# Latent attention: weights times values as one float32 product per key tile, with the sums in the same product

## Chip, cores and metric

The kernel runs on one core of a Trainium2 chip. What is compared is the device time of one execution in microseconds (us), the median of several runs.

## What is computed

The reference is a network of two blocks on 1024 tokens of width 1024. The change touches one part of the second block, an attention of eight heads ("latent", because its keys and values are made from a narrow projection). Each head has 1024 queries and keys of 96 numbers (64 plain, 32 rotated) and values of 64:

```python
def mla_attention(q, k, v):
    ...
    def one_block(q_blk):
        s = jnp.einsum('bqhd,bkhd->bhqk', q_blk, k).astype(jnp.float32) * scale
        p = jax.nn.softmax(s, axis=-1).astype(v.dtype)
        return jnp.einsum('bhqk,bkhd->bqhd', p, v)
    ...

def second_block(...):
    ...
    out_a = mla_attention(q, k, v).reshape(B, S, MLA_WIDTH)
    ...
    out_b = dilated_attention(partial_rope(dq), partial_rope(dk), dv.reshape(B, S, DIL_HEADS, DIL_HEAD_DIM))
    ...
    mixed = jnp.einsum('bsc,cd->bsd', jnp.concatenate([out_a, out_b], axis=-1), w_out[l])
    x = x + gt_a * mixed
    ...
    x = x + gt_m * expert_choice_ffn(h2, w_router[l], b_router[l], w_gate[l], w_up[l], w_down[l])
```

## The kernel before

**How the order comes about.** Every piece of work is a generator that issues some instructions and then yields a condition. `Sched.run` asks a record of what was issued so far (`Model`, with a planned clock for each engine) which piece goes next, by priority. The result is a fixed order of instructions for each of five queues: PE (products), DVE (vector), ACT (scalar, exponentials), POOL (GpSimd) and SP (which issues the transfers). Each queue runs in its order and waits on semaphores. All instructions are recorded on one line, L186, so the profile is read by tiles: `blk` is a 4 KB block of the on-chip heap, `hb` a 2 KB one, `ps` one of eight banks for products, `mmx` and `mng` the maxima of the latent attention and their negation, `mrd` the reciprocals of its sums.

**Precision.** A number is usually split into a high and a low part of type float32r (`copy` or `split` makes the high part, a subtraction the low one), and a product of two split operands is three products of parts (`mm3`). The profile shows float32r as f32 too. What tells the two apart there: a product in plain float32 stands as two records, each with its weight load.

**The latent attention** (`mla`, L2447). `mla_make` makes queries, keys and values and writes them to memory. `mla_keys`, `mla_vals` and `mla_queries` load them again and split them. Sixteen units (`mla_unit`, L2323; a head and half of the queries, so 512 queries against 1024 keys) do the rest, up to `MLIVE` = 6 of them begun at once, each with `MRES` = 6 blocks kept back for it:

1. eight products of high parts, 128 queries by 512 keys, whose maxima DVE takes (`top`); negated, they are transposed by four products and copied by ACT into row 96 of the queries, so that the next product subtracts them;
2. for each pair `j` of key tiles two times three products (128 keys by 512 queries, 97 rows with that of the maxima), whose exponentials ACT takes into `e`;
3. POOL adds the exponentials of all key tiles into `acc`, one 128x512 addition for each tile but the first;
4. `e` (128 x 1024) is split: a copy by ACT or DVE, and a subtraction by `lo_any` on DVE or POOL;
5. for each key tile two products with [high | low] values as weights (`mm2`), one pair behind (`MLAG` = 1), all sixteen into one bank;
6. the bank is copied to `ob`; four products of `acc` with ones give the sums, four products with two stacked identities (`fold`) transpose the result and add its halves; DVE takes the reciprocal and multiplies, and the result goes to memory.

The core of steps 3 to 5 before:

```python
            nc.gpsimd.tensor_add(acc, e[:, 0], e[:, 1]) if j == 0 else nc.gpsimd.tensor_add(acc, acc, e[:, 0])
            if j > 0:
                nc.gpsimd.tensor_add(acc, acc, e[:, 1])
            ...
            hl = [R.blk((P, 2, 512), F32R) for _ in range(2)]
            self.copy(hl[0], e)
            yield
            self.lo_any(hl[1], e, hl[0])
```

**What runs beside it.** The dilated attention (`dilated`, `dil_load`, `dil_unit`, `dil_merge`) has a lower priority and fills gaps, up to four of its units at once while the latent attention runs. When both are done, the output projection, the routing of tokens to experts and the experts follow.

Of the kernel before, what the change touches and what calls it, by code (L numbers as in the profile page):

```python
# [9 lines left out]
F32 = mybir.dt.float32  # L10
# [9 lines left out]
P = 128  # L20
# [16 lines left out]
MRES = 6  # L37
# [55 lines left out]
FE = 1000.0  # L93
# [14 lines left out]
# ---------------------------------------------------------------- the order of the instructions  # L108
class Model:
    """What the instructions issued so far occupy: it decides which piece of work is issued next."""  # L110
# [109 lines left out]
class Sched:  # L220
# [16 lines left out]
    def run(self):  # L237
        """until all but the background is done"""
# [122 lines left out]
# ---------------------------------------------------------------- memory and arithmetic  # L361
class Base:
# [70 lines left out]
    def copy(self, out, src):  # L433
        """on whichever of the two engines is free first"""
# [22 lines left out]
    def mm2(self, out, v, hi, lo, start, stop):  # L457
        """v = [high | low] of 64 columns: the parts of the sum end up in the two halves of the rows"""
# [24 lines left out]
    def bc_row(self, dst, row, n=1024):  # L483
        """every partition gets the row"""
# [16 lines left out]
    def lo_any(self, out, src, hi):  # L501
        """operands on chip: on whichever of the two engines is through first"""
# [7 lines left out]
class Reserve:  # L510
    """blocks kept back for a piece of work that has begun: it can always go on"""
# [32 lines left out]
class Weights:  # L544
    """Blocks of weights in the order of their use: loaded, then split in two float32r parts."""
# [71 lines left out]
class Block1(Base):  # L617
    # ---- start
# [65 lines left out]
    def mod_dve(self, l, js, wname, bname, wl, vecs):  # L684
        """weighted rows summed on the vector engine, then over the partitions on the tensor engine: 512 columns at a time"""
# [41 lines left out]
    def mod_pool(self, l, js):  # L727
        """rows weighted by the scalar engine and summed on GpSimd, both vectors: 512 columns at a time"""
# [42 lines left out]
    def scale(self, l, v, j, g):  # L771
        """g (1 + scale)"""
# [11 lines left out]
    # ---- norms and transposes of a tile  # L784
    def prenorm(self, x, A, B):
        """(x rstd) A + B"""
# [12 lines left out]
    def transpose_split(self, z, dst):  # L799
        """z [128, 1024] transposed; dst(half) lists (columns of the bank, hi, lo)"""  # L800
# [20 lines left out]
    # ---- projections into the mixer  # L821
# [9 lines left out]
    def proj(self, ps, xT, W, key, nk, n):  # L831
        """a token tile against a block of columns"""
# [19 lines left out]
    def f_evac(self, S, t, pf):  # L852
# [4 lines left out]
        else:  # L857
            # tokens half the sequence apart
# [10 lines left out]
    def f_parts(self, S):  # L869
        """the first steps of the transform over the eight tiles, in place"""  # L870
# [5 lines left out]
        # even: G0, G4, Re G2, -Im G2  # L876
# [6 lines left out]
        # odd: Re G3, Re G1, Im G3, -Im G1  # L883
# [12 lines left out]
    def ug_evac(self, S, t, pu):  # L896
        """twice the gelu; the gate's heads normed"""
# [42 lines left out]
    # ---- spatial gating  # L940
# [23 lines left out]
    def sgu(self, S):  # L964
        """u (w v + b) / 2, in place of u"""
# [22 lines left out]
    # ---- Fourier  # L988
# [8 lines left out]
    def fourier(self, S):  # L997
# [32 lines left out]
        else:  # L1030
# [12 lines left out]
            # part, offset in the table [S | C | -S | -C]: a real part takes [C | -S], an imaginary one [S | C]  # L1043
# [82 lines left out]
    # ---- attention  # L1126
# [10 lines left out]
    def rope(self, out, tmp, src, t, heads):  # L1137
        """out = src cos + swapped src (signed) sin, over heads of 64"""
# [93 lines left out]
    def unit(self, S, C, t, kv, st):  # L1232
        """4 heads of a query tile"""
# [190 lines left out]
    def post(self, x, ys, G):  # L1424
        """x + rmsnorm(y) G, in place of x"""
# [32 lines left out]
    def out_proj(self, seqs, W, l, src, dst):  # L1458
        """merge, project, add to the residual, norm for the feed-forward"""
# [88 lines left out]
    # ---- feed-forward  # L1548
# [22 lines left out]
    def ff(self, seqs, W, groups, fin, last_group):  # L1571
        """all the tokens against a group of chunks of the hidden width at a time"""
# [75 lines left out]
    def finisher(self, S, l, src, dst, nxt):  # L1648
        """after the feed-forward: residual, and the next norm"""
# [33 lines left out]
    # ---- the block  # L1683
# [68 lines left out]
    def start_mods(self, done):  # L1752
        """scale and shift of the first norms: one on the tensor engine, the other on the vector engine; on every partition"""
# [73 lines left out]
    def start(self, X, C):  # L1827
        """the modulation of the first norms; the tiles of the input"""
# [127 lines left out]
class Block2(Block1):  # L1956
    """proj, latent attention, dilated attention, experts"""

    # ---- rotations from the positions
    def tables2(self):  # L1960
# [14 lines left out]
        def cosine(out, r, tmp):  # L1975
            """sin(pi / 2 - |r|)"""
# [4 lines left out]
        # tokens on the partitions: [cos (32 | 16) | sin, signed]  # L1981
# [22 lines left out]
        # rows 64..95: cosines, 96..127: signed sines; the tokens along the free dimension  # L2004
# [18 lines left out]
    # ---- projections  # L2023
# [35 lines left out]
    def c_evac(self, nm, t, ps):  # L2059
        """norm of a latent, transposed"""  # L2060
# [44 lines left out]
    def passes2(self, X, W):  # L2105
# [19 lines left out]
        for b in range(KB):  # L2125
            for i in range(2):
                k = self.kbuf[b][i]
                self.nc.vector.tensor_scalar(k[96:97, :], self.tabT[96:97, :], 0.0, 1.0 - i, op0=OP.mult, op1=OP.add)
# [5 lines left out]
    # ---- latent attention  # L2134
# [1273 lines left out]
```

## Time and profile before

| | us |
|---|---|
| median of three runs (4331.38 to 4336.57) | 4331.73 |
| span of the profiled execution, first to last instruction | 4329.5 |
| from the first maximum of the latent attention to its last result | 3023 to 3397 |
| rest of the dilated attention, first part of the output projection | 3397 to 3585 |
| end of the output projection, router | 3585 to 3666 |
| sorting for the routing, then gathering the first tokens | 3666 to 3715 |
| experts, end | 3715 to 4329 |

The profiled execution stands in the profile with its span alone; what lies around the span in a run is the difference to the median, 2.2 us. The stages are read from the trace: the maxima `mmx` start at 3023.2 and the last multiplication by `mrd` starts at 3396.9, the last product of the dilated attention with `dw` starts at 3582.6, and the first token gather starts at 3715.1. A view by stages gives for each the busy time of every engine and the granted clock of PE as a share of full speed. A busy PE is not a PE at its peak: its records overlap, and their ends are modelled.

### The profile page before, as it was taken

What the parts mean: (1) busy time and instruction counts of PE and PEld (TensorE: products, weight loads), DVE (VectorE), ACT (ScalarE), POOL (GpSimd) and SP (SyncE); (2) the same over time, 40 slices, a digit from 0 to 9 for tenths busy, and PEclk for the clock granted to TensorE, in tenths of its full rate; (3) what the DMA queues carried; (4) which work ended last, traced back from release to release, by engine and by line L of the source; (5) the groups of instructions that cost most, each with busy time, mean ns of one, the idle gap of its engine ahead of it and who ended that gap; (6) DMA issues with size and microseconds to landing.
All of it is one profiled execution on the core that took longest, in us unless ns stands there. A gap on an engine that the chain in (4) does not pass through costs nothing. (4 is left out here: it accounts for less than half of the span.)

```text
span 4329.5 us, 54977 instructions
## 1 busy us (share of the span) xinstructions
PE 4034.2 (93%) x19984; PEld 3295.4 (76%) x19984; DVE 2780.2 (64%) x5030; ACT 1825.5 (42%) x3699; POOL 769.1 (18%) x853
## 2 busy tenths in 40 slices
PE   7998999999999979989999999798888898699997
PEld 3777778878887869878888888687676787587776
DVE  6447875666666385777233333814788776888898
ACT  3236643221221233564321222413455653687876
POOL 2111130000000061212000000401567424100001
PEclk8999999999999989999999999899889899799999
DMA  6202322233434240133111112423211345799998
GB/s 220 88 23 79 122 81 89 84 103 118 129 116 126 79 148 22 40 122 112 44 45 44 59 44 81 132 70 95 65 34 30 93 128 195 278 350 369 380 368 304
DMA packets 318761, 552.98 MB, mean 128 GB/s; under 512 B 93117, under 2 KB 177365, under 8 KB 318490
## 3 DMA queue, kind: packets, MB, share of 16 engines
q1 hardware_dynamic: 309130, 515.39, 34.9%
q0 software_dynamic: 9360, 34.08, 2.8%
q8 instruction: 157, 2.57, 0.2%
q14 instruction: 114, 0.93, 0.1%
HBM read 488.42 MB, written 60.97 MB: 127 GB/s over the span
## 5 line engine op out<-in xcount | busy, mean ns | idle before, releaser
L186 PE MATMUL ps<-blk 128*128 128x512 f32 (+3 forms) x16104 | 3542.5, 377 | 84.1 <-DVE blk L186 55.8
L186 PEld LDWEIGHTS ps<-blk 128*128 128x128 f32 (+1 forms) x16104 | 2847.1, 192 | 654.4 <-DVE blk L186 87.6
L186 DVE TENSOR_TENSOR blk<-blk 128x1024 fp32r<-128x1024 f32 (+7 forms) x808 | 922.9, 1182 | 139.1 <-ACT blk L186 126.0
L186 ACT CAST blk<-blk 128x1024 fp32r<-128x1024 f32 (+3 forms) x679 | 661.2, 1022 | 662.3 <-DMA blk<-in_w_ff_dram 390.3
L186 DVE TENSOR_TENSOR blk<-blk,ps 128x512 f32<-128x512 f32 (+1 forms) x488 | 324.8, 675 | 326.5 <-PE ps L186 324.9
L186 ACT CAST blk<-ps 128x512 fp32r<-128x512 f32 (+5 forms) x608 | 275.0, 480 | 441.7 <-PE ps L186 420.9
L186 PE MATMUL ps<-ident,blk 128*128 128x128 f32 (+1 forms) x2024 | 327.9, 296 | 113.6 <-DVE blk L186 53.4
L186 POOL TENSOR_TENSOR blk<-blk 128x1024 f32<-128x1024 f32 (+3 forms) x120 | 252.9, 2113 | 1004.4 <-DMA blk<-in_g_post_ff_dram 647.0
L186 DVE TENSOR_TENSOR blk<-ps,blk 128x512 fp32r<-128x512 f32 (+7 forms) x702 | 349.7, 532 | 108.9 <-ACT blk L186 83.1
L186 PEld LDWEIGHTS ps<-ident,blk 128*128 128x128 f32 x2024 | 261.8, 161 | 178.1 <-ACT blk L186 52.0
L186 ACT ACTIVATE hb<-ps 128x512 f32<-128x512 f32 (+2 forms) x194 | 106.5, 549 | 523.3 <-PE ps L186 512.5
L186 DVE SCALAR_TENSOR_TENSOR hb<-hb,cT 128x512 f32<-128x512 f32 x224 | 164.2, 749 | 112.5 <-DMA hb<-in_w_ada_dram 111.0
L186 ACT ACTIVATE blk<-blk,z 128x256 f32<-128x256 f32 (+2 forms) x406 | 214.4, 532 | 46.3 <-DVE z L186 41.3
L186 DVE CAST blk<-hb 128x512 fp32r<-128x512 f32 (+2 forms) x127 | 48.9, 389 | 262.6 <-ACT hb L186 258.0
L186 ACT ACTIVATE blk<-ps 128x512 f32<-128x512 f32 (+1 forms) x198 | 117.4, 598 | 187.6 <-PE ps L186 182.8
L186 ACT ACTIVATE hb<-hb 128x512 f32<-128x512 f32 (+5 forms) x386 | 176.1, 484 | 37.8 <-DVE hb L186 16.8
L186 ACT ACTIVATE blk<-blk 128x1024 f32<-128x1024 f32 (+4 forms) x157 | 117.4, 751 | 162.7 <-DVE blk L186 141.8
L186 ACT COPY blk<-ps 128x512 f32<-128x512 f32 (+2 forms) x131 | 77.2, 596 | 250.5 <-PE ps L186 250.4
L186 POOL TENSOR_TENSOR hb<-hb,blk 128x512 f32<-128x512 f32 x96 | 170.1, 1771 | 26.6 <-ACT blk L186 20.4
L186 DVE SCALAR_TENSOR_TENSOR blk<-blk,z 128x1024 f32<-128x1024 f32 (+2 forms) x146 | 155.0, 1095 | 21.1 <-POOL z L186 20.3
L186 DVE CAST blk<-ps 128x512 fp32r<-128x512 f32 (+2 forms) x178 | 93.5, 545 | 106.1 <-ACT blk L186 53.3
L186 POOL TENSOR_SCALAR sinkb<-sinkb 128x8 f32<-128x8 f32 x2 | 0.5, 245 | 888.8 <-DMA sinkb<-in_sink_dram 888.8
(150 smaller groups left out, 2060.6 us busy)
## 6 DMA issues: line engine op xcount, KB each, us to landing
blk<-in_w_ff_dram SPq DMA_DIRECT2D x128, 512.0 KB
blk<-in_w_gate_dram SPq DMA_DIRECT2D x128, 512.0 KB
blk<-in_w_up_dram SPq DMA_DIRECT2D x128, 512.0 KB
blk<-in_w_down_dram SPq DMA_DIRECT2D x128, 512.0 KB
hb<-in_w_ada_dram SPq DMA_DIRECT2D x208, 256.0 KB
blk<-in_w_ada_dram SPq DMA_DIRECT2D x40, 512.0 KB
blk<-in_w_in_dram SPq DMA_DIRECT2D x36, 512.0 KB
xd<-blk SPq DMA_DIRECT2D x32, 512.0 KB
```

The lines of the kernel that those rows point to most:

```text
L186: return f(*a, **k)
```

## The change

The exponentials are not split. Each key tile takes one float32 product, with the values as weights (66 columns: 64 values and two columns of ones), and row 64 of the result holds the sums. So `acc` and its additions, the split of `e`, the split of the values, the products with ones and the folds go; four transposes of 66 rows take the place of the folds. The values come by heads, eight transfers instead of four, up to four heads ahead. The low parts of queries and keys no longer have a row 96 (the second and third product of the scores read 96 rows), so the clearing of that row by POOL goes. A unit keeps three blocks back instead of six, and counts as ended (`st["live"]`) a step earlier.

```diff
-MRES = 6
+MRES = 3
...
 def mla_vals(self):
...
-            vs = [R.blk((P, 8, 2, 64), F32R) for _ in range(2)]
-            for h, v in enumerate(vs):
-                self.copy(v[:, :, 0], f[:, :, h * 64:(h + 1) * 64])
-            yield
-            for h, v in enumerate(vs):
-                self.lo_any(v[:, :, 1], f[:, :, h * 64:(h + 1) * 64], v[:, :, 0])
...
+        for h in range(8):
+            yield lambda: self.vn == 8 and h < self.hfree + 4 and self.room(2)
+            v = self.blk((P, 8, 66))
+            nc.sync.dma_start(v[:, :, 0:64], self.vd[:, h * 64:(h + 1) * 64].rearrange("(t p) c -> p t c", p=P))
+            nc.vector.memset(v[:, :, 64:66], 1.0)
+            yield
+            self.vm.append(v)
...
 def mla_queries(self):
...
-                nc.gpsimd.memset(q[96:97, 1].bitcast(F32), 0.0)
...
 def mla_unit(self, h, half, st, R):
...
-        acc = self.hb()
...
-            if i == 0:
-                return
-            nc.gpsimd.tensor_add(acc, e[:, 0], e[:, 1]) if j == 0 else nc.gpsimd.tensor_add(acc, acc, e[:, 0])
-            if j > 0:
-                nc.gpsimd.tensor_add(acc, acc, e[:, 1])
-            if self.whole(FE):
-                pend[j] = [e]
-                return
-            yield lambda: R.room(2)
-            hl = [R.blk((P, 2, 512), F32R) for _ in range(2)]
-            self.copy(hl[0], e)
-            yield
-            self.lo_any(hl[1], e, hl[0])
-            R.free(e)
-            yield
-            pend[j] = hl
+            if i:
+                pend[j] = e
...
-                    self.mm3(ps, tuple(x[0:97, k] for x in kb), tuple(x[0:97, :] for x in qb), True, True)
+                    for n, (x, y, m) in enumerate(((0, 0, 97), (0, 1, 96), (1, 0, 96))):
+                        nc.tensor.matmul(ps, kb[x][0:m, k], qb[y][0:m, :], start=n == 0, stop=n == 2)
...
-                    if len(hl) == 1:
-                        nc.tensor.matmul(po, v.bitcast(F32), hl[0][:, i], start=x == 0, stop=x == 7)
-                    else:
-                        self.mm2(po, v, hl[0][:, i], hl[1][:, i], x == 0, x == 7)
-                R.free(*hl)
+                    nc.tensor.matmul(po[:66, :], self.vm[h][:, x], e_[:, i], start=x == 0, stop=x == 7)
+                R.free(e_)
...
-        self.copy(ob, po)
+        self.copy(ob[:66, :], po[:66, :])
         self.unbank(po)
+        st["live"] -= 1
+        yield
+        yield lambda: self.banks(2)
         pd = self.bank()
         for i in range(4):
-            nc.tensor.matmul(pd[:, 256 + 2 * i:258 + 2 * i], acc[:, i * P:(i + 1) * P], self.ones, start=True, stop=True)
-        self.freeh(acc)
+            nc.tensor.transpose(pd[:, i * P:i * P + 66], ob[:66, i * P:(i + 1) * P], self.ident[:66, :66])
         yield
         rd = self.sm(4, "mrd", 3)
-        nc.vector.reciprocal(rd, pd[:, 256:264].rearrange("p (i q) -> p i q", q=2)[:, :, 0])
-        for i in range(4):
-            self.fold(pd[:, i * 64:(i + 1) * 64], ob[:, i * P:(i + 1) * P])
-        st["live"] -= 1
...
+        pv = pd.rearrange("p (i c) -> p i c", c=P)
+        nc.vector.reciprocal(rd, pv[:, :, 64])
```

**Where instructions move.** The order of every engine is the same as before up to the first unit's maxima, and again from the sorting on; between them the scheduler, which reckons a float32 product at twice the time of two float32r ones, makes another order. On PE, around the unit of head 4 and second half, before: the four transposes of its maxima, then its scores (`blk`, three for each key tile) mixed with products with values (`blk`, four for a pair of key tiles) of its own and of the unit before it, whose products with ones (`ones,hb`) and folds (`ident_76,hb`) stand between, and transposes of the dilated attention (`identr,blk`).

```order
L186 MATMUL ps<-ident,mng 1x128 x4
L186 MATMUL ps<-blk 128x512 x5
L186 MATMUL ps<-identr,blk 128x128 x8
L186 MATMUL ps<-blk 128x512 x17
L186 MATMUL ps<-ones,hb 128x2 x4
L186 MATMUL ps<-blk 128x512 x3
L186 MATMUL ps<-ident_76,hb 128x64 x4
L186 MATMUL ps<-blk 128x512 x22
L186 MATMUL ps<-ident,mng 1x128 x4
L186 MATMUL ps<-blk 128x512 x20
```

The same place after: `66x512` are the float32 products with values, `ident,hb 128x66` the new transposes, `128x256` and `ident,blk` the dilated attention.

```order
L185 MATMUL ps<-ident,mng 1x128 x4
L185 MATMUL ps<-ident,blk 128x128 x8
L185 MATMUL ps<-blk 128x512 x13
L185 MATMUL ps<-blk 66x512 x2
L185 MATMUL ps<-blk 128x512 x6
L185 MATMUL ps<-blk 66x512 x2
L185 MATMUL ps<-blk 128x512 x6
L185 MATMUL ps<-blk 66x512 x4
L185 MATMUL ps<-blk 128x512 x5
L185 MATMUL ps<-ident,hb 128x66 x4
L185 MATMUL ps<-blk 128x512 x2
L185 MATMUL ps<-blk 128x256 x8
```

A unit's scores and its products with values now stand in one row, with no other unit's between them; the maxima of the next two units, the transposes of the result and pieces of the dilated attention stand at the seam between two units.

On POOL, in the same part of the program, before: additions into `acc` (`hb<-hb,blk`, and `hb<-blk` for a unit's first), clearing of row 96 (MEMSET), and the rotation of the queries (`32x512`).

```order
L186 TENSOR_TENSOR hb<-blk 128x512
L186 TENSOR_TENSOR hb<-hb,blk 128x512 x2
L186 TENSOR_TENSOR hb<-hb 32x512
L186 TENSOR_TENSOR hb<-hb,blk 128x512 x4
L186 MEMSET blk 1x512
L186 TENSOR_TENSOR blk<-blk 128x8x64
L186 TENSOR_TENSOR hb<-hb 32x512
L186 TENSOR_TENSOR hb<-blk 128x512
L186 TENSOR_TENSOR blk<-blk 128x8x64
L186 TENSOR_TENSOR hb<-hb,blk 128x512 x6
```

The same part after, with splits of the queries (`96x512`) and of the dilated attention's values (`128x8x64`):

```order
L185 TENSOR_TENSOR blk<-hb,blk 96x512
L185 TENSOR_TENSOR hb<-hb 32x512
L185 TENSOR_TENSOR blk<-hb,blk 96x512
L185 TENSOR_TENSOR blk<-blk 128x8x64
L185 TENSOR_TENSOR hb<-hb 32x512
L185 TENSOR_TENSOR blk<-hb,blk 96x512
```

The seven additions of each unit are gone from POOL, and what is left is two short instructions for each unit and the dilated attention's splits.

## Rows read from the trace of the kernel before

**Rows 1.** Stages; us; PE, PEld, DVE, ACT, POOL busy (instructions); granted clock; DMA; GB/s.
```profile
2060.00:2690.00 630.00, 630.00 (x2781) 521.65 (x2780) 195.75 (x266) 144.32 (x203) 0.30 (x1) 1.00 0.16 50
...
3023.00:3397.00 374.00, 319.02 (x1461) 251.16 (x1461) 301.53 (x441) 204.58 (x367) 240.15 (x150) 0.89 0.17 41
3397.00:3585.00 188.00, 173.37 (x1127) 157.70 (x1127) 142.21 (x414) 111.80 (x303) 53.28 (x31) 0.91 0.49 137
3585.00:3666.00 81.00, 79.18 (x437) 67.37 (x438) 54.79 (x132) 29.43 (x59) 37.17 (x28) 0.97 0.53 191
...
3715.00:4329.00 614.00, 577.82 (x2712) 467.63 (x2712) 537.72 (x579) 473.15 (x619) 61.81 (x50) 0.98 0.93 346
```

**Rows 2.** Waits in 3023 to 3397: engine, for whom; total us, times, longest.
```profile
PEld ps L186 <- DVE blk L186: 46.8, 41, 4.5
PE ps L186 <- DVE blk L186: 32.2, 29, 4.1
...
PE ps L186 <- DVE mrd L186: 10.5, 9, 2.5
```

**Rows 3.** Groups of 3023 to 3397: DVE, ACT and POOL work; busy us, mean ns.
```profile
L186 POOL TENSOR_TENSOR hb<-hb,blk 128x512 f32<-128x512 f32 x96 | 170.1, 1771 | 26.6 <-ACT blk L186 20.4
L186 DVE TENSOR_TENSOR blk<-blk 128x1024 fp32r<-128x1024 f32 x67 | 112.6, 1685 | 9.9 <-ACT blk L186 9.4
...
L186 DVE TENSOR_REDUCE mmx<-ps 128x1 f32<-128x512 f32 x128 | 82.4, 678 | 6.9 <-PE ps L186 6.7
...
L186 ACT ACTIVATE blk<-ps 128x512 f32<-128x512 f32 x128 | 75.7, 598 | 85.2 <-PE ps L186 81.6
L186 ACT CAST blk<-blk 128x1024 fp32r<-128x1024 f32 x50 | 52.1, 1047 | 0.7
...
L186 POOL TENSOR_TENSOR hb<-blk 128x512 f32<-128x512 f32 x16 | 25.3, 1581 | 70.0 <-ACT blk L186 57.6 <-issue 8.0 <-DMA hb<-mq 4.2
```

**Rows 4.** DVE's costliest group in 2060 to 2690, where POOL is idle.
```profile
L186 DVE TENSOR_TENSOR blk<-blk 128x1024 fp32r<-128x1024 f32 x58 | 69.8, 1223 | 57.7 <-ACT blk L186 57.7
```

**Rows 5.** PE in order of time, two kinds of products, 512 columns: start, us, records.
```profile
79.67 5.31 PE L186 MATMUL ps<-blk,cT 128*2 128x512 f32 x12
84.91 3.01 PE L186 MATMUL ps<-blk 128*128 128x512 f32 x12
```

**Rows 6.** Groups of PE in 3023 to 3397: records, busy us, mean ns.
```profile
L186 PE MATMUL ps<-blk 128*128 128x256 f32 x112 | 22.0, 333 | 0.0
L186 PE MATMUL ps<-ident,hb 128*128 128x64 f32 x128 | 21.7, 325 | 10.6 <-DVE mrd L186 10.5
L186 PE MATMUL ps<-ones,hb 128*128 128x2 f32 x128 | 18.0, 263 | 3.1 <-POOL hb L186 3.1
```

**Rows 7.** PE in order of time, the small products: start, us, records.
```profile
3250.96 0.95 PE L186 MATMUL ps<-ones,hb 128*128 128x2 f32 x8
3251.77 0.94 PE L186 MATMUL ps<-blk 97*128 97x512 f32 x3
...
3405.98 3.77 PE L186 MATMUL ps<-ident,blk 128*128 128x64 f32 x32
...
3409.90 0.62 PE L186 MATMUL ps<-ident,blk 128*128 128x128 f32 x4
3410.28 0.54 PE L186 MATMUL ps<-identr,blk 128*128 128x128 f32 x4
...
3412.56 2.16 PE L186 MATMUL ps<-blk 128*128 128x256 f32 x16
3414.55 0.80 PE L186 MATMUL ps<-identr,blk 128*128 128x128 f32 x8
```

**Rows 8.** Two tiles' own views: ns least/median/most, of all instances.
```profile
L186 PE MATMUL ps<-blk,cT x128: 592/592/1061, 6.3 to 248.6; 128*2 128x512 f32 x128
...
L186 DVE TENSOR_TENSOR mng<-mmx x16: 131/154/1245, 3050.3 to 3361.0; 128x4 f32<-128x4 f32 x16
...
L186 DVE TENSOR_TENSOR hb<-ps,mrd x16: 410/425/425, 3079.7 to 3396.9; 128x256 f32<-128x256 f32 x16
```

More of the change, by code (lines that the diff above doesn't have):

```diff
@@ L92 @@
 DQ = 3.0
-FE = 1000.0
 FT = 2.0
@@ L2127, in passes2 @@
                 k = self.kbuf[b][i]
-                self.nc.vector.tensor_scalar(k[96:97, :], self.tabT[96:97, :], 0.0, 1.0 - i, op0=OP.mult, op1=OP.add)
+                if i == 0:
+                    self.nc.vector.tensor_scalar(k[96:97, :], self.tabT[96:97, :], 0.0, 1.0, op0=OP.mult, op1=OP.add)
                 if b > 0:
@@ L2284, in mla_vals @@
         nc = self.nc
-        for pr in range(4):
-            yield lambda: self.vn == 8 and 2 * pr < self.hfree + 3 and self.room(3)
-            R = self.reserve(3)
-            f = R.blk((P, 8, P))
-            nc.sync.dma_start(f, self.vd[:, pr * P:(pr + 1) * P].rearrange("(t p) c -> p t c", p=P))
-            yield
-            vs = [R.blk((P, 8, 2, 64), F32R) for _ in range(2)]
-            for h, v in enumerate(vs):
-                self.copy(v[:, :, 0], f[:, :, h * 64:(h + 1) * 64])
-            yield
-            for h, v in enumerate(vs):
-                self.lo_any(v[:, :, 1], f[:, :, h * 64:(h + 1) * 64], v[:, :, 0])
-            self.free(f)
-            R.close()
-            yield
-            self.vm += vs
+        for h in range(8):
[3 more added lines that the diff above has]
+            nc.vector.memset(v[:, :, 64:66], 1.0)
+            yield
+            self.vm.append(v)
     def mla_queries(self):
@@ L2362, in mla_unit @@
         pend = {}
-        yield lambda: self.roomh(1)
-        acc = self.hb()
         def expo(ps, e, i, j):
@@ L2401, in mla_unit @@
                     po = self.bank()
-                hl = pend.pop(j - MLAG)
+                e_ = pend.pop(j - MLAG)
                 for i in range(2):
                     x = 2 * (j - MLAG) + i
-                    v = self.vm[h][:, x].rearrange("p a d -> p (a d)")
-                    if len(hl) == 1:
-                        nc.tensor.matmul(po, v.bitcast(F32), hl[0][:, i], start=x == 0, stop=x == 7)
-                    else:
-                        self.mm2(po, v, hl[0][:, i], hl[1][:, i], x == 0, x == 7)
-                R.free(*hl)
+                    nc.tensor.matmul(po[:66, :], self.vm[h][:, x], e_[:, i], start=x == 0, stop=x == 7)
+                R.free(e_)
                 yield 0
@@ L2420, in mla_unit @@
         yield
-        pr = h // 2
         yield lambda: self.roomh(1) and self.banks(2)
         ob = self.hb()
-        self.copy(ob, po)
+        self.copy(ob[:66, :], po[:66, :])
         self.unbank(po)
+        st["live"] -= 1
+        yield
+        yield lambda: self.banks(2)
         pd = self.bank()
         for i in range(4):
-            nc.tensor.matmul(pd[:, 256 + 2 * i:258 + 2 * i], acc[:, i * P:(i + 1) * P], self.ones, start=True, stop=True)
-        self.freeh(acc)
+            nc.tensor.transpose(pd[:, i * P:i * P + 66], ob[:66, i * P:(i + 1) * P], self.ident[:66, :66])
         yield
         rd = self.sm(4, "mrd", 3)
-        nc.vector.reciprocal(rd, pd[:, 256:264].rearrange("p (i q) -> p i q", q=2)[:, :, 0])
-        for i in range(4):
-            self.fold(pd[:, i * 64:(i + 1) * 64], ob[:, i * P:(i + 1) * P])
-        st["live"] -= 1
-        yield
-        nc.vector.tensor_mul(ob[:, 0:256].rearrange("p (q d) -> p q d", d=64), pd[:, 0:256].rearrange("p (q d) -> p q d", d=64),
-                             rd[:, :, None].to_broadcast([P, 4, 64]))
+        pv = pd.rearrange("p (i c) -> p i c", c=P)
+        nc.vector.reciprocal(rd, pv[:, :, 64])
+        nc.vector.tensor_mul(ob[:, 0:256].rearrange("p (q d) -> p q d", d=64), pv[:, :, 0:64], rd[:, :, None].to_broadcast([P, 4, 64]))
         self.unbank(pd)
```

1 line of the change is left out of this document (removed).

## Prediction

> **What bounds the kernel now.** I read the stages first, then who waits for whom, then single groups. The table of stages [rows 1] shows where the change lies: from 3023 to 3397 us, 374 us long. In 2060 to 2690 PE is busy all the time at a granted clock of 1.00; in the 374 us it is busy for 319.0, DVE for 301.5, POOL for 240.2, ACT for 204.6, at a clock of 0.89. So neither PE nor DVE fills the stage: PE waits 55 us in all. What it waits for is mostly DVE: 32.2 us on PE and 46.8 on its weight loads (the two overlap) end with a `blk` that DVE wrote, a low part [rows 2]. And DVE is slow there: a 128x1024 subtraction takes 1685 ns [rows 3], against 1223 ns in the stage in which POOL does nothing [rows 4]. The subtraction of two four-number columns `mng<-mmx` shows the same: 131 ns at the least, 1245 at the most [rows 8]. I read this as DVE held up while POOL works, above all on its additions into `acc`.
>
> The stage's PE work at full clock, worked out to compare with afterwards. A 512-column float32r product takes 630/2781 = 0.2265 us [rows 1]. By the program there are 867 of them (16 units of 8 + 24 + 16, and 99 for the queries): 196.4. The 136 narrower ones of the dilated attention (112 of them are the row in [rows 6]) cost 1.99/16 = 0.124 [rows 7]: 16.9. The 128 records with ones [rows 6] cost 0.81/8 = 0.10 [rows 7]: 13.0. Folds: 128 records [rows 6] and 18 of the dilated attention at 3.77/32 = 0.118 [rows 7]: 17.2. The 200 transposes cost 0.38/4 = 0.095 [rows 7]: 19.0. Sum 262.5 us. So 111 of the 374 us are lost, 55 as idle time, some 41 to the clock (11% of 374), the rest in the ends of products before waits.
>
> **The change part by part.**
>
> *Products with values.* For each of 128 key tiles (16 units of 8) two float32r products, 2 x 0.2265 = 0.453, become one float32 product. The trace has such products: 512 float32 columns with weights of two columns, two records for each, 12 records in 84.91 - 79.67 = 5.24 us [rows 5], so 0.873 a product. That is 0.420 more, times 128: **+53.8 us of PE work**. From below this is firm, since 512 columns stream in both. From above, weights of 66 columns might not load behind the records; the bound is the median of a single record, 592 ns [rows 8], 1.184 a product, +39.8 us more. I take the stream, since 128-column weights load behind 0.2265 us products without a gap in 2060 to 2690 [rows 1]. [...]
>
> *Sums and folds.* The records with ones go, -13.0. The 128 fold records (15.1) become 64 transposes (6.1): -9.0. The transposes of 66 rows have no row; at the price of a fold record they would cost 1.5 more, which I leave to the range. PE's work so rises by 53.8 - 13.0 - 9.0 = **+31.8**.
>
> *Split and additions.* DVE loses nearly all 64 subtractions, 64 x 1.685 = 108, and the 15 copies that ACT did not take; ACT loses 49 copies of 1.047, 51 us; POOL loses 112 additions, 170.1 + 25.3 = 195 us [rows 3]. What stays is under 180 us for DVE, 155 for ACT, 40 for POOL. None of this comes off the time by itself: it takes away what PE waited for, and PE with some 300 us becomes the bound.
>
> *Small edits in one go.* Eight value loads instead of four, and eight clearings of two columns on DVE: the stage's DMA share is 0.17 [rows 1], and values come up to four heads ahead, so nobody waits; at zero cover each load would cost a few us, once. The clearing of row 96 leaves POOL. The 96 rows instead of 97 I take as nothing, since the 512 columns stay. Fewer reserved blocks let more of the dilated attention in.
>
> *The order.* It moves dilated work into the stage: by the program 24 float32r transposes, 24 folds and 12 instructions of dilated units, 2.3 + 5.7 + 1.3 = 9.3 us of PE. And 24 products of the output projection (5.4 us) fall behind the dilated attention's end.
>
> *The seam.* A unit's scores and products with values now stand without another unit's between. ACT keeps up inside: eight exponentials of 0.598 = 4.8 us [rows 3] beside 24 x 0.2265 + 8 x 0.873 = 12.4 us of PE. [...] PE has 3 to 5 us of its own in most seams (maxima of the next units, transposes, dilated products). I take 2 us of loss for a unit, idle time and ends of products together: 32 us. It lies between 0.5, if all is covered, and 4, if nothing is. The clock I take at 0.97: 10 us; it was 0.97 in 3585 to 3666 with PE busy 98% and 0.91 in 3397 to 3585 with 92% [rows 1].
>
> **The sum.** The stage then lasts 262.5 + 31.8 + 9.3 + 32 + 10 = 345.6, against 374: -28.4. The next stage, 188 us, loses 9.3 + 5.4 = 14.7 of PE work; it takes 188/173.4 us for each busy one [rows 1], so -16. The output projection's 24 products come back behind it: +5.4. After that the order is unchanged, and the experts (577.8 of 614 us PE, DMA 0.93 [rows 1]) only begin earlier. Together **-39 us**, on a span of 4329.5, which lies 2.2 us under the median of the runs, 4331.7. I predict 4293 us.
>
> **Rivals.**
>
> *The clock stays at 0.89.* For it: the loss to the clock does not follow the busy share alone, and the seams' transposes and short products are still there. Then the stage loses 303.6/0.89 - 303.6 = 37.5 us to the clock instead of 10: 4293 + 27 = 4320. [...] Against it: twelve us of products without a break in each unit.
>
> *The seam is not covered; slower.* One mechanism: the next unit's maxima are reduced on DVE (0.678 each [rows 3]) behind the dilated attention's work, and PE, with nothing of another unit's to do, waits for the negated maximum. Before, two units' products lay mixed and covered this. The price is up to 6 us a seam, 96 instead of 32: 4293 + 64 = 4357. It turns the result slower from 374 + 10.6 - 303.6 - 10 = 71 us, 4.4 us a unit. For it: order and waits are fixed by planned times, not by real ones. Against it: DVE, with under 180 us of work in 346, is rarely behind.
>
> *The float32 product costs more.* With weight loads not hidden, up to 1.184 each, +39.8 us: 4333, no change. For it: the row has weights of two columns. Against it: see above.
>
> **How the numbers follow.** Forecast 0.64, clock 0.16, seam 0.10, dear product 0.10. A measurement of this kernel can tell about 0.2% (8.7 us) from no change: faster is under 4323. The forecast gives 0.62 of faster and the clock rival 0.10, the dear product, which is not likely to cost its whole bound, 0.02: 0.74. Within 0.2%: 0.14, from the rest of these. Slower: the seam and a little of the dear product, 0.12. The range reaches from 4264 (seams wholly covered and a full clock, -29) to 4332, just short of the dear product's end; out of it are the seam rival and the tails, 2 in 10.
>
> **What would show it.** In the changed profile: the records of `66x512` start 0.44 us apart (not 0.59); no additions on POOL, and 128x1024 subtractions nearly gone from DVE; maxima to last multiplication by `mrd` about 346 us (over 385 would be the seam); granted clock there near 0.97 rather than 0.89; PE's waits for DVE's `blk` under 20 us, its waits at the seams (for `mng`, for ACT's row) 1 to 2 us a unit; sorting begins some 39 us earlier, and the experts' stage still lasts 614 us. The prediction is wrong in its core if PE is busy under 85% of that stage.

## Result: 4274.5 us, 1.4% faster; the profile after

The changed kernel takes 4274.45 us (median of four runs, 4273.72 to 4281.4). The kernel before, run beside it, took 4334.15 (4331.38 to 4343.1). The ratio is 0.986, with a 95% interval from 0.9847 to 0.9873, so -60 us; the profiled spans differ by 57.4 (4329.5 and 4272.1). Forecast were -39.

Stages of the changed kernel (us; then busy time and instructions of PE, PEld, DVE, ACT and POOL; the granted clock; DMA share; GB/s). They answer to the last four rows of [rows 1]; the sorting, left out there, is left out here too ("...").

```profile
3018.60:3354.60 336.00, 321.15 (x1361) 204.49 (x1359) 157.16 (x381) 163.88 (x333) 42.11 (x33) 0.99 0.22 52
3354.60:3525.30 170.70, 153.97 (x1012) 140.69 (x1010) 129.58 (x386) 104.88 (x295) 42.95 (x24) 0.92 0.49 131
3525.30:3609.00 83.70, 81.44 (x434) 68.50 (x435) 57.60 (x127) 29.29 (x57) 35.90 (x27) 0.98 0.60 206
...
3658.50:4272.00 613.50, 577.12 (x2712) 466.90 (x2712) 537.35 (x579) 472.94 (x619) 61.72 (x50) 0.98 0.93 346
```

The latent stage is 38 us shorter, and what PE does in it has turned round: 321.15 of 336.00 us busy at a clock of 0.99, instead of 319.0 of 374 at 0.89. So PE's idle time falls from 55 to 15 us, and what the clock costs (the missing share times the stage) from some 41 to 3 us: about as much comes back through the clock as through the idle time itself. DVE's busy time is about half of before, POOL's a sixth. The experts' stage has the length it had.

Waits of PE and of its weight loads in the latent stage after (us in total, times, longest), in answer to [rows 2]; "issue" is time with no wait that the profile shows (PE is idle for 15 us in all, so some 45 of these 59.8 or more pass while PE is busy):

```profile
PE ps L185 <- ACT blk L185: 11.0, 11, 1.7
PE ps L185 <- DVE blk L185: 1.6, 3, 0.7
...
PE ps L185 <- DVE mng L185: 0.3, 1, 0.3
...
PEld ps L185 <- issue: 59.8, 212, 0.6
PEld ps L185 <- ACT blk L185: 32.3, 71, 2.2
PEld ps L185 <- DVE blk L185: 3.3, 9, 1.0
```

PE's wait for DVE's `blk` is down to 1.6 us, and 3.3 for its weight loads; it was 32.2 and 46.8. What is waited for now is a `blk` of ACT, eleven times on PE and 11 us in all.

Groups of the same stretch (busy us, mean ns of one; idle time before, and what ended it), in answer to [rows 3], [rows 6] and [rows 8]:

```profile
L185 PE MATMUL ps<-blk 128*66 128x512 f32 x256 | 118.1, 593 | 0.0
...
L185 DVE TENSOR_REDUCE mmx<-ps 128x1 f32<-128x512 f32 x128 | 81.6, 682 | 114.2 <-PE ps L185 114.0
...
L185 DVE TENSOR_TENSOR hb<-ps,mrd 128x256 f32<-128x256 f32 x16 | 6.8, 425 | 1.7 <-DVE mrd L185 0.2
```

The 256 records of the first row are the 128 float32 products. DVE waits for PE, 114 us before the maxima alone; before, PE waited for DVE. What a float32 product costs in the row is read from a timeline of PE (start, us from the first start to the last end, records):

```profile
3184.09 12.72 PE L185 MATMUL ps<-blk 97*128 97x512 f32 x40
3196.65 0.60 PE L185 MATMUL ps<-ident,mng 128*1 128x128 f32 x4
```

One unit's scores and products with values, without a break: 24 records of scores and 16 of float32 products, begun 3184.09 and followed at 3196.65, so 12.56 us. With 24 x 0.2265 = 5.44 for the scores, 7.12 us remain for 16 records: 0.445 each, 0.89 a product. The 66-row transposes go four in 0.22 us:

```profile
3174.78 0.42 PE L185 MATMUL ps<-ident,hb 66*128 66x66 f32 x4
3175.00 0.94 PE L185 MATMUL ps<-blk 96*128 96x512 f32 x3
```

### The profile page after: what moved, and what is told of

It reads as the page before. It is cut to its first block, busy times and chain, and to the rows that moved or that the text cites. A ratio compares the mean times of both kernels' runs of the same rounds, so it can differ in the third digit from the quotient of the medians.

```text
span 4272.1 us, 54181 instructions
## 1 busy us (share of the span) xinstructions
PE 4026.4 (94%) x19792; PEld 3240.1 (76%) x19792; DVE 2620.3 (61%) x4945; ACT 1776.9 (42%) x3648; POOL 552.9 (13%) x723
## 5 line engine op out<-in xcount | busy, mean ns | idle before, releaser
L185 DVE TENSOR_TENSOR blk<-blk 128x1024 fp32r<-128x1024 f32 (+8 forms) x743 | 815.4, 1139 | 142.0 <-ACT blk L185 135.7
L185 ACT CAST blk<-blk 128x1024 fp32r<-128x1024 f32 (+2 forms) x625 | 608.1, 1025 | 658.6 <-DMA blk<-in_w_ff_dram 370.2
L185 ACT CAST blk<-ps 128x512 fp32r<-128x512 f32 (+4 forms) x610 | 276.8, 482 | 423.2 <-PE ps L185 404.7
L185 POOL TENSOR_TENSOR blk<-blk 128x1024 f32<-128x1024 f32 (+3 forms) x113 | 240.1, 2129 | 1050.4 <-PE ps L185 664.6
L185 DVE CAST blk<-hb 128x512 fp32r<-128x512 f32 (+3 forms) x130 | 49.8, 387 | 260.2 <-ACT hb L185 255.6
L185 DVE CAST blk<-ps 128x512 fp32r<-128x512 f32 (+3 forms) x176 | 91.5, 539 | 105.7 <-ACT blk L185 53.2
L185 DVE TENSOR_REDUCE mmx<-ps 128x1 f32<-128x512 f32 x128 | 81.6, 682 | 114.2 <-PE ps L185 114.0
L185 DVE TENSOR_TENSOR blk<-hb,blk 128x512 fp32r<-128x512 f32 (+5 forms) x224 | 122.1, 557 | 39.4 <-ACT blk L185 36.5
```

Source lines behind the costliest of these rows:

```text
L185: return f(*a, **k)
```

## The experiments

Each kernel ran beside the kernel before, which took 4334 to 4337 us. All times are medians; ratios are to that kernel. "PE's work" is the program's instructions at the prices of [rows 1, 5 to 7], with 0.89 for the float32 product. Three points cut the profiled spans: the first `mmx`, the end of the last multiplication by `mrd`, and the first gather of tokens for the experts. The stretch from the first point to the last is 691.9 us long before and 640.0 after: -51.9.

**The product alone, with POOL's additions left.** The kernel before already has a switch for it:

```diff
-FE = 1000.0
+FE = -1000.0
```

> The kernel before with one part of the change alone: the exponentials are not split, and each key tile takes one float32 product with the [high | low] values; the additions on POOL, the products with ones and the folds stay. Theory A (the split on DVE held PE up; PE bounds the stage without it): most of the gain is there, the records with ones (13 us) and the folds (9 us) still to pay, so 4295 to 4305 us, and the stage some 360 us. Rival B (POOL's additions were the brake, through the DVE instructions that they held up): little gain, 4320 to 4350.

Measured: 4330.79 us, ratio 0.9988 (0.9978 to 0.9998). That is no gain to speak of; the rival had it. The split is gone from DVE and ACT, and the stretch is nearly as long as before (687.4 us): PE has 56 us more to do, and only about as much was won. In the latent stage PE's idle time falls from 55 to 23 us, and the clock rises from 0.89 to 0.94, which is worth some 20. So the float32 product without the columns of ones is not worth its price.

**The additions alone.**

```diff
-            nc.gpsimd.tensor_add(acc, e[:, 0], e[:, 1]) if j == 0 else nc.gpsimd.tensor_add(acc, acc, e[:, 0])
-            if j > 0:
-                nc.gpsimd.tensor_add(acc, acc, e[:, 1])
+            if j == 0:
+                nc.gpsimd.memset(acc, 8.0)
```

> The kernel before without POOL's 112 additions: the array of sums is set to a constant by one instruction a unit, so the result is not divided by the sums; all else stays, split and two products too. Theory A: DVE's 128x1024 subtractions go from 1.69 to about 1.22 us, 30 us off DVE, of which a part reaches PE: 4305 to 4325 us. Rival B: most of the gain, 4280 to 4295, with PE's waits for DVE's blocks under 30 us.

Measured: 4290.56 us, ratio 0.9887 (0.9871 to 0.9904): -45 us. The split, which PE's waits had named, is still there; only POOL's additions are gone. The theory that asked for 4305 to 4325 missed, the rival had it. DVE's groups in the latent stage (3028 to 3347 us here) show one reason:

```profile
L186 DVE TENSOR_TENSOR blk<-blk 128x1024 fp32r<-128x1024 f32 x59 | 76.0, 1291 | 15.6 <-ACT blk L186 15.0
```

The subtraction takes 1291 ns instead of 1685 [rows 3], and PE's waits for DVE's low parts fall to 10.7 us (weight loads 17.6):

```profile
PE ps L186 <- DVE blk L186: 10.7, 10, 3.2
...
PEld ps L186 <- DVE blk L186: 17.6, 21, 3.6
```

**The split alone, with no float32 product.** ACT writes the exponentials as float32r, and both products read them; PE's work stays.

```diff
...
-            hl = [R.blk((P, 2, 512), F32R) for _ in range(2)]
-            self.copy(hl[0], e)
-            yield
-            self.lo_any(hl[1], e, hl[0])
-            R.free(e)
-            yield
-            pend[j] = hl
+            pend[j] = [e, e]
...
-                e = R.blk((P, 2, 512))
+                e = R.blk((P, 2, 512), F32R)
...
```

> The kernel before without the split, at the same PE work: ACT writes the exponentials as float32r, and both products of a key tile take them (the low part is left out, and the high one counted twice, so the result is doubled). POOL's additions, the products with ones and the folds stay. Theory A, as it stands after the first runs (the time is PE's work plus what PE loses; without the split it loses some 59 us less, which the float32 product then spends): 4265 to 4290 us. Rival B (the additions themselves are the brake, not the split): 4315 or more.

Measured: 4345.49 us, ratio 1.0024 (1.0014 to 1.0034): 10 us slower. The work that the waits had named is taken away, and nothing comes of it: the first theory asked for at most 4290. The latent stage of this kernel (3025 to 3406 us) has as much idle PE as before, 55 us, and a lower clock, 0.85; its waits tell where the time went:

```profile
3025.00:3406.00 381.00, 326.15 (x1448) 266.50 (x1448) 160.47 (x354) 158.29 (x316) 188.57 (x152) 0.85 0.16 39
...
PE ps L186 <- POOL hb L186: 39.2, 16, 3.3
...
PEld ps L186 <- POOL hb L186: 45.9, 16, 3.7
```

Sixteen waits, one for each unit, for the accumulator. Timelines of POOL and of PE over one unit of this kernel (start, us, operation; in brackets the idle time before and what ended it):

```profile
3180.67 1.29 POOL L186 TENSOR_TENSOR hb<-blk 128x512 f32<-128x512 f32 x1 [2.94 <-ACT blk L186]
3182.04 8.08 POOL L186 TENSOR_TENSOR hb<-hb,blk 128x512 f32<-128x512 f32 x6
...
3176.63 11.10 PE L186 MATMUL ps<-blk 128*128 128x256 f32 x52
3190.17 1.05 PE L186 MATMUL ps<-ones,hb 128*128 128x2 f32 x8 [2.44 <-POOL hb L186]
```

POOL adds seven times without a pause, 1.35 us each, and ends at 3190.12. PE is through with the products with values 2.44 us earlier and cannot go on: its next instruction is the product with ones, and behind it in the fixed order stand the folds, the products for the maxima of a coming unit, and then the next unit's scores.

The same place in the kernel before, one seam, on POOL, DVE and PE:

```profile
3172.76 8.88 POOL L186 TENSOR_TENSOR hb<-hb,blk 128x512 f32<-128x512 f32 x4 [0.95 <-ACT blk L186]
...
3178.99 1.50 DVE L186 TENSOR_TENSOR blk<-blk 128x1024 fp32r<-128x1024 f32 x1
...
3180.55 0.98 PE L186 MATMUL ps<-blk 128*128 128x512 f32 x3 [0.32 <-DVE blk L186]
3181.70 1.05 PE L186 MATMUL ps<-ones,hb 128*128 128x2 f32 x8 [0.17 <-POOL hb L186]
```

The unit ends in two tails side by side. DVE's last low part is ready at 3180.49 and lets PE's last products go at 3180.55; POOL's last addition ends at 3181.64, and PE's products with ones start at 3181.70. After the wait for the first tail only 0.17 us are left of the second, and so the waits name DVE. Not every seam is like this one: by the same trace the sum is ready less than 0.7 us before the products with ones in eight of the sixteen, and 1.9 to 6.9 us before them in the others.

**Neither split nor additions, PE's work as before.**

```diff
-            nc.gpsimd.tensor_add(acc, ef[0], ef[1]) if j == 0 else nc.gpsimd.tensor_add(acc, acc, ef[0])
-            if j > 0:
-                nc.gpsimd.tensor_add(acc, acc, ef[1])
+            if j == 0:
+                nc.gpsimd.memset(acc, 8.0)
```

(on the kernel without the split)

> The kernel before with neither the split nor the additions, at its PE work: exponentials as float32r, counted twice by the two products, the sums set to a constant by one instruction a unit. So the result is doubled and not divided by the sums. Theory E (after a unit's last exponentials two tails of some 3 us run side by side, the split on ACT and DVE and the last two additions on POOL, and PE waits for the later one, so that either alone hides what the other's removal would bring): far more than the removal of the split alone (which brought nothing) and more than that of the additions alone (45 us): 60 to 85 us off, 4250 to 4275. Rival B (only the additions count): as without the additions, 4283 to 4298.

Measured: 4276.05 us, ratio 0.986 (0.9843 to 0.9876): -61 us against the kernel before, where the split alone gave +10. The time is a microsecond above the theory's range and 7 us under the rival's. In the latent stage PE's idle time falls from 55 us without the split to 26, and the clock rises from 0.85 to 0.93, which is worth some 34 us. By these rows more than half of what the waits at the seams cost is clock:

```profile
3026.00:3351.10 325.10, 299.27 (x1480) 243.26 (x1481) 155.60 (x358) 160.10 (x321) 51.47 (x59) 0.93 0.20 48
```

**The last two additions of a unit alone.** On the same kernel without the split, five of POOL's additions and a clearing stay; only those of the last pair of exponentials go.

```diff
-            nc.gpsimd.tensor_add(acc, ef[0], ef[1]) if j == 0 else nc.gpsimd.tensor_add(acc, acc, ef[0])
-            if j > 0:
-                nc.gpsimd.tensor_add(acc, acc, ef[1])
+            if j < 3:
+                nc.gpsimd.memset(acc, 1.0) if j == 0 else nc.gpsimd.tensor_add(acc, acc, ef[0])
+                nc.gpsimd.tensor_add(acc, acc, ef[1])
```

> The kernel before without its split (ACT writes the exponentials as float32r, both products read them), and of POOL's seven additions a unit only five and a clearing, those of the first three pairs: nothing is added after the last pair of exponentials, so the sums leave out a quarter of the keys and the product is doubled. PE's work is that of the kernel before. Theory E (PE waits at a unit's end for whichever of two tails comes last: the split of the last pair or POOL's two additions of it): with both tails gone PE's 39 + 46 us of waiting for POOL's sum, as seen without the split alone, mostly go: 4285 to 4310. Rival F (it is the mass of POOL's additions that holds up DVE and so PE, wherever they stand): five of seven additions remain, so little changes: 4320 to 4330 or more.

Measured: 4271.88 us, ratio 0.985 (0.9833 to 0.9867): 74 us less than with all seven, more than the theory asked for, with 80 of 112 additions in place. PE's waits for POOL, 3026 to 3290 us of this kernel, and the additions there:

```profile
PE ps L186 <- POOL hb L186: 0.9, 1, 0.9
...
PEld ps L186 <- POOL hb L186: 1.4, 1, 1.4
...
L186 POOL TENSOR_TENSOR hb<-hb,blk 128x512 f32<-128x512 f32 x80 | 106.3, 1329 | 63.6 <-ACT blk L186 58.1
```

That the mass of additions costs the time, wherever they stand, falls as the main cause in the kernel without the split: it is when the sum is ready. With the split, where the additions do slow DVE (1685 ns a subtraction instead of 1291), it stays open how much of the 45 us of the additions alone came from DVE's faster subtractions and how much from the sum. A reservation: the scheduler, which makes a new order for each of these kernels, reckons with the earlier end, and has the dilated attention nearly all behind the latent stage (PE's work in that stage 235 us instead of 260). But the whole stretch from the first maximum to the first gather, which holds the same work in every order, went from 701.7 us to 631.1.

**Is PE the bound after?** One float32r product for a key tile in place of the float32 one; the low parts of exponentials and values are left out.

```diff
-            v = self.blk((P, 8, 66))
...
+            f = self.blk((P, 8, 66))
...
+            v = self.blk((P, 8, 66), F32R)
+            self.copy(v, f)
...
-                e = R.blk((P, 2, 512))
+                e = R.blk((P, 2, 512), F32R)
```

> The changed kernel with float32r exponentials and values, so that each key tile takes one float32r product instead of one float32 product (the low parts are left out, a less exact result). PE loses 128 x (0.89 - 0.2265) = 85 us of work, DVE or ACT gains eight copies. Theory A (PE bounds the stage): 60 to 80 us come off, 4195 to 4215 us. Rival D (the seams, ACT or DVE bound it by now): 30 us or less, 4245 or more.

Measured: 4194.06 us, ratio 0.9669 (0.9653 to 0.9685). PE has 128 x (0.89 - 0.2265) = 85 us less to do, and the time falls by 80. PE bounds the stage. (The stage itself is 115 us shorter; some 18 us of that are work of the dilated attention that moved behind it.) This version beats both kernels, with exponentials and values rounded to float32r, which both kernels avoid. Its latent stage:

```profile
3016.00:3237.30 221.30, 212.13 (x1064) 165.61 (x1065) 143.99 (x332) 141.96 (x289) 37.85 (x29) 1.00 0.28 69
```

**Blocks kept back for a unit.** The prediction priced `MRES` at nothing. The changed kernel with the old value:

```diff
-MRES = 3
+MRES = 6
```

> The changed kernel with six blocks kept back for a unit again, instead of three. Theory A: no difference, 4270 to 4280 us, since the seams are filled by what the order has at hand. Rival C (the room for the dilated attention makes the dense order): 10 to 20 us slower, with more idle PE at the seams.

Measured: 4303.71 us, ratio 0.9921 (0.9905 to 0.9938): 29 us slower than with 3, by the medians half of the whole gain, and more than either expectation had. In the profiled executions the stretch from the first maximum to the first gather is 661.8 us long instead of 640.0, so 22 us of it lie where the two kernels differ. The latent stage itself is shorter. PE waits hardly more in it than with 3 (16.9 us in all instead of 14.0), but 7.9 of them now for the negated maxima:

```profile
3022.00:3337.00 315.00, 297.01 (x1177) 181.55 (x1176) 138.32 (x312) 148.02 (x285) 41.24 (x31) 0.98 0.20 50
...
PE ps L185 <- DVE mng L185: 7.9, 6, 3.1
```

But 20.8 us of the dilated attention's PE work are done behind the stage instead. The stage gives back no more than that work, 20.9 us, and from its end to the first gather it takes 346.9 us instead of 304.2: 42.7 us more for 20.8 us of work. In these two kernels this work costs its bare time at the seams of the units and about twice that behind them.

Is 3 worth as much without the change? The kernel before with `MRES = 3`, and the product alone with it:

> The kernel before with three blocks kept back for a unit instead of six, nothing else. Theory A (more of the dilated attention in the stage helps only where PE has seams to fill and DVE has time): 4325 to 4345 us, no difference. Rival C (the room for the dilated attention is worth its 20 to 30 us by itself): 4303 to 4315 us.

> The kernel before with unsplit exponentials and one float32 product, as in the first run of this study, and three blocks kept back instead of six. Theory A: the room is worth about what it is worth in the changed kernel, some 29 us, so 4296 to 4308 us; what is left to the changed kernel is the products with ones and the folds, 22 us of PE. Rival (the room does nothing here): 4325 to 4335 us.

Measured: 4327.54 us (ratio 0.9991, 0.998 to 1.0002) and 4331.92 (0.9989, 0.9978 to 1.0). Neither is to be told from the kernel before, nor the second from the product alone with 6; the 4296 to 4308 that were expected of the second missed. In the kernel before, the room brings 23 us of dilated work into the latent stage, which grows by 21, as in the changed kernel; but what follows gets only 28.6 us shorter, not 42.7. Why it is less there is not shown. Between the second of these kernels and the changed one the stretch falls by 50 us (690.1 to 640.0): 24.6 are PE's work, and which of the other edits brings the rest was not tried. And still less:

> The changed kernel with MRES = 1 instead of 3: still fewer blocks reserved for a unit of the latent attention, so more room for the dilated attention's blocks at the seams. If room is what made 3 worth 29 us against 6 (each block some 10 us): faster by 5 to 20, 4255 to 4269. If the room that 3 leaves was already enough for the seams, or blocks taken away from the latent units make them wait for blocks: 4272 to 4290.

Measured: 4285.95 us, ratio 0.9882 (0.9863 to 0.9901): not faster, and 11 us over the median with 3, though the intervals of the two ratios overlap. More of the dilated attention goes into the stage (PE's work 313.7 us instead of 303.0), but the whole stretch is 643.1 us long instead of 640.0. Three was room enough; whether one is worse stays open.

**POOL's additions in the changed kernel, for nobody.**

```diff
+        acc = self.hb()
...
+            nc.gpsimd.tensor_add(acc, e[:, 0], e[:, 1]) if j == 0 else nc.gpsimd.tensor_add(acc, acc, e[:, 0])
+            if j > 0:
+                nc.gpsimd.tensor_add(acc, acc, e[:, 1])
...
+        self.freeh(acc)
```

> The changed kernel with POOL's 112 additions put back; nobody reads their sum. Theory A (additions cost time only through the DVE instructions of the split, which are gone): within 6 us of the changed kernel, 4270 to 4281 us. Rival B (additions hold blocks or DVE whatever else runs): 20 to 40 us slower, 4294 or more.

Measured: 4288.93 us, ratio 0.989 (0.9874 to 0.9907), 14 us over the changed kernel. PE waits for POOL nowhere, and yet the latent stage is 359.6 us long instead of 335.8. Since the planner reckons with the additions, PE's order is another one: 57.6 us of dilated work in the stage instead of 41.1. So once more with the additions left out of the planner's account, and the order that of the changed kernel, on PE, DVE and ACT, as the two traces show:

```diff
-            nc.gpsimd.tensor_add(acc, e[:, 0], e[:, 1]) if j == 0 else nc.gpsimd.tensor_add(acc, acc, e[:, 0])
+            nc.gpsimd._r.tensor_add(acc, e[:, 0], e[:, 1]) if j == 0 else nc.gpsimd._r.tensor_add(acc, acc, e[:, 0])
...
-                nc.gpsimd.tensor_add(acc, acc, e[:, 1])
+                nc.gpsimd._r.tensor_add(acc, acc, e[:, 1])
```

> The changed kernel with POOL's 112 additions into an accumulator that nobody reads, as in the run with the additions put back, but left out of the planner's account, so that PE's instructions stand in the order of the changed kernel. Theory G (the 14 us that the additions cost there came from another order: dilated work pulled into the stage that PE had to do at its pace): within 5 us of the changed kernel, 4270 to 4280, the latent stage 333 to 340 us long. Rival H (POOL's additions themselves hold up DVE or ACT, and PE behind them): 4284 to 4295, the latent stage longer by 8 us or more with the same PE work.

Measured: 4282.91 us (4275.7 to 4284.23), ratio 0.9874 (0.9854 to 0.9893), between the two expectations. The latent stage is as long as in the changed kernel, 336.1 us from the first maximum on, with POOL busy for 187.70 us in it:

```profile
3019.00:3357.90 338.90, 323.23 (x1373) 206.75 (x1371) 163.38 (x382) 164.73 (x334) 187.70 (x145) 0.99 0.22 54
```

So 112 additions that nobody waits for cost the stage nothing (first maximum to first gather: 643.0 us instead of 640.0, against 654.2 with the other order). The median's 8 us over the changed kernel lie where the intervals of the two ratios overlap; of the profiled span's 8.0, 3.0 stand ahead of the first maximum. Whether anything of it is real stays open.

## Why the prediction was right, and where not

*The bound changes from waits to PE.* Right: PE busy 321 of 336 us, at 0.99. The run with less of PE's work shows it. In the latent stage PE's idle time falls by 40 us and its loss to the clock by 38, against 40.6 us more of PE's work (31.3 and 9.3). Why PE had waited was read too narrowly. "What it waits for is mostly DVE" is true of the wait's name. But without the split PE waited as long for POOL's sum. What the split and the additions cost does not add up (+10 us without the one, -45 without the other, -61 without both): they end side by side, nearly so in half of the seams, and the later one counts. That the forecast held in spite of this reading was luck: the change takes away both. A rough sum over the runs agrees: -61 for both and +31.3 of PE's work make -30, and the changed kernel with the old reserve is 32 us faster than the kernel before; the rest came with the reserve.

*Products with values:* forecast +53.8 us, measured 0.89 a product instead of 0.873, 128 x (0.89 - 0.453) = +55.9. The weights of 66 columns do load behind the records (0.445 in the row, beside 593 ns for a single one, which was the upper bound), and the rival of the dear product falls. A float32 product took 3.9 times the 0.2265 us of a float32r one.

*Sums and folds:* forecast -22.0. The transposes cost 0.055 each instead of 0.095, so -13.0 - 15.1 + 3.5 = -24.6. PE's work rises by 31.3; forecast 31.8.

*The latent stage:* forecast 345.6 us, measured 335.8. DVE has 157 us to do there (under 180 forecast), ACT 164 (155) and POOL 42 (40). The two mis-sized terms are the clock and, a little, the seam. The clock was taken at 0.97, 10 us; it is 0.99 [rows 1 have 0.89], about 3. PE's work, 303 us, and the clock leave 30 us for seams and ends of products, 1.9 a unit; 2 were forecast, the author's estimate. No run shows its limits of 0.5 and 4; what the runs show in their place is the 1.9. The clock's rival, which kept 0.89, and the seam's, 4.4 a unit and more, did not come: the maxima on DVE wait for PE, and PE waits for `mng` once, 0.3 us. With the old reserve it did so for 7.9 us, so a little of that rival was in reach. The lower end of the range, 4264, is 5 us too high by its own terms: seams at 0.5 us a unit are -24 and a full clock -10, together -34 and not -29. Nothing hangs on it. The seams' transposes, which the clock's rival named, did not hold the clock down: it is 0.99 in the stage with 64 transposes of results and 64 of maxima in it. That they could was not shown.

*The stages around it.* The first maximum is reached 4.4 us earlier, which was not forecast, with the copies and low parts of the values no longer ahead of it; that this is the cause was not tried, and over the profiled runs this point lies between 3016.1 and 3026.0 in kernels made from the changed one and between 3022.0 and 3028.0 in the others. From the last multiplication by `mrd` to the first gather it takes 304.2 us instead of 317.8: -13.6, where -16 and +5.4, together -10.6, were forecast. The experts' stage: -1.1 (forecast 0). The sum is -38.3 - 4.4 - 13.6 - 1.1 = -57.4, forecast -39.

*"Fewer reserved blocks let more of the dilated attention in"* had no number, and that is the gap in the working: the reserve is worth 22 to 29 us of the gain in the changed kernel, though no difference can be told in the kernel before. The forecast took the order as the scheduler makes it, with 9.3 us more of the dilated attention in the stage, so its sum did not suffer; but it did not see that this order hung on the reserve.

## What to carry to other kernels

The engine that a wait names need not be the only one that is late: before, PE waited 32.2 us for DVE's `blk` [rows 2], and with the split gone 39.2 us for POOL's sum. Before taking work off it, look in the timeline for what ends in the microsecond after, and price the removal by that. And idle time is not the whole price of a wait: in these kernels the clock about doubled it (40 us of idle time and 38 of clock between before and after, 29 and 34 between the kernel without the split and that with neither). Taking both tails away at equal work (here -61 us) tells what there is to gain, and so how much work on the bounding engine the change may add. A number that reserves room belongs to the sum as well as an instruction does: run the change with the old number.

## What the hardware showed

In these kernels DVE and POOL held each other up when both worked in SBUF. The 128x1024 subtraction takes 1223 ns with POOL idle [rows 4], 1291 with POOL's additions gone, 1685 beside them [rows 3]. The other way, POOL's addition of 512 columns takes 1771 ns beside the split [rows 3] and 1297 when the split is gone, as the group in the kernel without the split shows:

```profile
L186 POOL TENSOR_TENSOR hb<-hb,blk 128x512 f32<-128x512 f32 x96 | 124.5, 1297 | 8.3 <-ACT blk L186 0.9
```

Not every instruction of DVE was held up. In the changed kernel with the additions in the same order, the tile view of the maxima (duration ns least/median/most, first and last start, forms) has:

```profile
L185 DVE TENSOR_REDUCE mmx<-ps x128: 673/681/693, 3021.8 to 3328.0; 128x1 f32<-128x512 f32 x128
L185 DVE TENSOR_TENSOR mng<-mmx x16: 148/153/1246, 3045.4 to 3329.8; 128x4 f32<-128x4 f32 x16
```

No reduction out of PSUM takes over 693 ns here, with POOL busy for 187.70 of 338.90 us; a subtraction of four columns with both inputs in SBUF takes up to 1246. What holds it up need not be an addition into `acc`: in the changed kernel, which has none, one of 843 ns (from 3276.74) ended 0.02 us after a 128x512 subtraction on POOL (3276.27, 1.29 us). With the additions gone from the kernel before the longest takes 2122, in a stage in which POOL still does eight 128x1024 subtractions, 2492 ns each.

```profile
L186 DVE TENSOR_TENSOR mng<-mmx x16: 131/154/2122, 3055.2 to 3319.6; 128x4 f32<-128x4 f32 x16
```

In the traces of the kernels before and after, 9 of the 32 subtractions `mng<-mmx` take over 200 ns, and each of the 9 ends some 0.02 us after the end of a POOL instruction that was running when it began. Two inputs are not the only case here. A `TENSOR_SCALAR` with one input, in the kernel before, began with a POOL instruction and ended with it:

```profile
3224.98 1.28 DVE L186 TENSOR_SCALAR mng<-mng 128x4 f32<-128x4 f32 x1
...
3224.97 1.26 POOL L186 TENSOR_TENSOR blk<-blk 128x512 fp32r<-128x512 f32 x1 [4.15 <-ACT blk L186]
```

Its median is 170 ns. Yet in the changed kernel with the additions in the same order the additions cost the stage nothing (336.1 us instead of 335.8), since DVE, busy for 163.38 of 338.90 us, had time to spare.
